# Hybrid GDN and retention block: GpSimd issues the stores of the latent chunks' preparation and of the adaLN rows

## The chip, the cores and the metric

One Trainium2 chip, one of its cores. The metric is the device time of one execution in microseconds; the time of a kernel is the median of its runs. Engines are called as in the profile: PE is TensorE (PEld its weight loads), DVE is VectorE, ACT is ScalarE, POOL is GpSimd, SP is SyncE, which does no arithmetic and only issues transfers (SPq is its queue).

## What is computed

One layer of a diffusion transformer over 256 context and 1024 latent tokens with 1024 features in float32. Cut to what matters here:

```
p = modulate(rms_norm([ctx; x])) @ w_in            # adaLN: shift, scale, gate from silu(c) @ W + b
q, k, v = silu(short_conv(p))                       # 4 heads of 128: gated DeltaNet (GDN)
decay[i, j] = exp(G[i] - G[j])        for i >= j    # G: running sum of the log decays in a chunk
A = strict_lower(beta_i * (k_i . k_j) * decay)      # per chunk, head and direction
u, w = solve(I + A, [beta v, beta k exp(G)])        # the triangular solve of each chunk
qk = (q_i . k_j) * decay ;  q_dec = q * exp(G)      # "scores" of the chunk
scan over chunks, forwards and backwards:  v_new = u - w S ;  o = q_dec S + qk v_new ;  S = ...
y = [GDN out ; retention out], gated ;  x += g1 * (y @ w_out)
x += g2 * swiglu(modulate(rms_norm(x))) ;  out = rms_norm(x)
```

The reference uses chunks of 64, the kernel chunks of 128 tokens; context chunks need no scores, since only latent tokens are put out.

## The kernel before

Products run on PE as three matmuls of float32 operands that are split into a high and a low part (whi, wlo; ACT L344 makes the high part, DVE or POOL L345 the low part). A scheduler orders the instructions of each engine when the program is built: each engine then works through its queue strictly in that order, and waits at an instruction until the semaphores it needs are there. All transfers that SP, ACT and POOL issue stand in their queues among the other instructions.

The program goes through these stages: adaLN and the norms; the in-projection, part of it with tokens on the partitions (`token_major`, matmuls L371 to L373), and for GDN's k, q and v with channels on the partitions (`conv_block`, L607 to L624, its convolution on DVE L621); then, per chunk of 128 tokens, the preparation and the triangular solves; the scan (`step`, first matmuls L922); retention; the out-projection; the feed-forward part; the last norm.

The change is in two places. `ada_rest` (L488) runs beside the projections of q and k, one call a head: SP loads the weights (L495), DVE accumulates, and for the two gate rows g1 and g2 SP loads a bias row (L503), DVE adds (L505), and SP stores 512 elements to the DRAM tile `grow` (L506). The row is read again much later, at 681 us (g1) and 1293 us (g2).

`pre(t)` (L700) prepares chunk t; there are 10, 0 and 1 of the context, 2 to 9 latent. Chunk rows kc and qc are loaded by SP (L664). PE makes kk = k k' and kq = k q' in PSUM. For each of two directions d, SP loads the decay row broadcast over the partitions (gw, L718), POOL masks it (e, `affine_select`, L722), ACT takes exp (L726), DVE multiplies kk by e into ut (L730) and, for latent chunks, kq by e into half of sp (L732). SP stores ut (128x512, 256 KB) to the DRAM tile un of its batch (L733). For latent chunks ACT takes exp of gw (L735), POOL multiplies it by qc into the other half of sp (L736), and SP stores sp (512 KB) to the scan's DRAM tile sd (L737). The tiles gw, e, ut and sp have two buffers each, so a store must have landed before DVE or POOL may write the tile again two directions later.

`BATCH = [[0,1,2,9],[3,8,4,7],[5,6]]` gives three batches of chunks. After the chunks of a batch, `invert(b)` (L743) inverts the 32x32 diagonal blocks: SP loads them from un into yr (L751), ACT and DVE copy them into L (L758, L759), DVE does 31 steps of a product and a subtraction (L765, L767) in series, copies a transpose (L769), and SP stores the results to xd (L771). `merge(b)` (L801) then builds the whole inverses: SP loads un into U (L783) and the diagonal blocks from xd into U (L787) and t64 (L788), PE multiplies (L807, L814, L817, L830, L834) with copies by DVE between (xt1 L810, xt2 L831) and by ACT. ACT stores U to sd (L838). The program text calls solve(0), solve(1) (preparation and inversion of batches 0 and 1), the convolution of v with its transposes (PE L856, ACT L859 into vt of two buffers, ACT store L860), the preparation of batch 2, merge(0), the load of the rope tables (L872), invert(2), merge(1), merge(2), and two `token_major` groups (8, 9), whose matmuls fill PE in this stage. The scheduler interleaves all of these.

```
for d in range(2):
    ...
    V.tensor_tensor(ut ..., pk, e ..., ALU.mult)                       # L730
    if t >= 2:
        V.tensor_tensor(sp[:, 0] ..., pq, e ..., ALU.mult)             # L732
    SY.dma_start(un[b][:, 1 - d, c * H:(c + 1) * H, :], ut)            # L733
```

Of the kernel before, what the change touches and what calls it, by code (L numbers as in the profile page):

```python
# [25 lines left out]
H = 4  # L26
# [12 lines left out]
def build(nc, tc, ap, dbg=None, stop=None, marks=None):  # L39
    root = ExitStack()  # L40
    V, S, G, T, SY = nc.vector, nc.scalar, nc.gpsimd, nc.tensor, nc.sync
# [51 lines left out]
    def bank_b(name):  # L93
        return bank("pb", name)
# [47 lines left out]
    def softplus(pl, x, n, tag):  # L142

        a = pl.tile([P, n], F32, tag=tag + "a", name=tag + "a")
        s = pl.tile([P, n], F32, tag=tag + "s", name=tag + "s")
        q = pl.tile([P, n], F32, tag=tag + "q", name=tag + "q")
        V.scalar_tensor_tensor(a, x, -1.0, x, ALU.mult, ALU.max)
        S.activation(a, a, AF.Exp, scale=-1.0)
        V.tensor_scalar(s, a, 2.0, None, ALU.add)
        V.reciprocal(s, s)  # L150
        V.tensor_tensor(s, s, a, ALU.mult)
        V.tensor_tensor(q, s, s, ALU.mult)
        V.tensor_scalar(a, q, 1.0 / 19.0, None, ALU.mult)
        for k in (17, 15, 13, 11, 9, 7, 5, 3):
            V.scalar_tensor_tensor(a, a, 1.0 / k, q, ALU.add, ALU.mult)
        V.scalar_tensor_tensor(a, a, 1.0, s, ALU.add, ALU.mult)
        V.tensor_scalar(s, x, 0.0, None, ALU.max)
        V.scalar_tensor_tensor(s, a, 2.0, s, ALU.mult, ALU.add)
        return s
# [31 lines left out]
    try:  # L191
# [293 lines left out]
        grow = [dr.tile([1, D], F32, tag="grow%d" % i, name="grow%d" % i) for i in range(2)]  # L485

        def ada_rest(c, half):

            c0 = c * D + half * 512
            src = ap["ada2"][2 * (c - 2) + half]  # L490
            acc = R2.tile([P, 512], F32, tag="acc", name="acc", bufs=1)
            for k in range(KT):
                if k % 2 == 0:
                    w = R2.tile([P, 2, 512], F32, tag="adaw2", name="adaw2", bufs=2)
                    SY.dma_start(w, src[k // 2])  # L495
                if k == 0:
                    V.tensor_scalar(acc, w[:, 0], csl[:, k, 0:1], None, ALU.mult)
                else:
                    V.scalar_tensor_tensor(acc, w[:, k % 2], csl[:, k, 0:1], acc, ALU.mult, ALU.add)
            ps = bank_b("gr")  # L500
            if c in (2, 5):
                row = R2.tile([1, 512], F32, tag="row", name="row", bufs=1)
                SY.dma_start(row, ap["adarow"][c0:c0 + 512].unsqueeze(0))  # L503
                T.matmul(ps[:1, :], ones[:, 0:1], acc, start=True, stop=True)
                V.tensor_tensor(row, row, ps[:1, :], ALU.add)  # L505
                SY.dma_start(grow[0 if c == 2 else 1][:, half * 512:(half + 1) * 512], row)  # L506
            else:
                for k in range(4):
                    T.matmul(ps[:, 2 * k:2 * k + 2], acc[:, k * P:(k + 1) * P], ones[:, 0:2], start=True, stop=True)
                ks = slice(half * 4, half * 4 + 4)  # L510
                o = ada2[:, c - 3, ks]
                V.tensor_tensor(o, ps[:, 0:8].rearrange("p (k t) -> p k t", t=2)[:, :, 0],
                                adab[:, 8 * c + 4 * half:8 * c + 4 * half + 4], ALU.add)
                if c == 4:
                    V.scalar_tensor_tensor(o, o, 1.0, gffn[:, ks], ALU.add, ALU.mult)
# [19 lines left out]
        for g in range(2):  # L535
            ada_rest(2, g)
# [13 lines left out]
        sd = dr.tile([TT, P, 10, 512], F32, tag="sd", name="sd")  # L550
# [4 lines left out]
        def c8(t, d):  # L555
            return slice(t * 8 + d * 4, t * 8 + d * 4 + 4)
# [11 lines left out]
        sp = softplus(AB, av.rearrange("p a n -> p (a n)"), 2 * TT * 8, "sp")  # L568
# [3 lines left out]
        sp = sp[:, :TT * 8]  # L572
# [82 lines left out]
        for h in range(H):  # L655
            y = newy()
            conv_block(4 + h, y, False)
            ada_rest(3 + h // 2, h % 2)
            S.dma_start(kd[:, :, h, :].rearrange("t p j -> p t j"), y.rearrange("p (t j) -> p t j", j=P))
            kstat(h, y)  # L660

        def load(pl, src, tag, bufs, shape=(P, H, P)):
            x = pl.tile(list(shape), F32, tag=tag, name=tag, bufs=bufs)
            SY.dma_start(x, src)  # L664
            return x
# [11 lines left out]
        for h in range(H):  # L677
            y = newy()
            conv_block(h, y, True)
            if h < 2:  # L680
                ada_rest(5, h)
            S.dma_start(qd[:, :, h, :].rearrange("t p j -> p t j"),
                        y[:, NCTX:].rearrange("p (t j) -> p t j", j=P))
# [14 lines left out]
        un = [dr.tile([P, 2, len(ch) * H, P], F32, tag="un%d" % b, name="un%d" % b) for b, ch in enumerate(BATCH)]  # L698

        def pre(t):  # L700
            b, c = where[t]
            kc = load(GP, kd[t], "kc", 2)
            pk = bank_b("kk")
            for h in range(H):
                T.matmul(pk[:, h * P:(h + 1) * P], kc[:, h, :], kc[:, h, :], start=True, stop=True)
            if t >= 2:
                qc = load(GP, qd[t - 2], "qc", 2)
                pn = bank_b("qt")
                for h in range(H):
                    T.transpose(pn[:, h * P:(h + 1) * P], qc[:, h, :], ident)  # L710
                for h in range(H):
                    S.activation(pn[:, h * P:(h + 1) * P], pn[:, h * P:(h + 1) * P], AF.Square, accum_out=nq[:, t - 2, h:h + 1])
                pq = bank_b("kq")
                for h in range(H):
                    T.matmul(pq[:, h * P:(h + 1) * P], kc[:, h, :], qc[:, h, :], start=True, stop=True)
            for d in range(2):
                gw = GP.tile([P, H, P], F32, tag="gw", name="gw", bufs=2)
                SY.dma_start(gw.rearrange("p h i -> p (h i)"),  # L718
                             grow_d[c8(t, d), :].rearrange("a b -> (a b)").partition_broadcast(P))
                e = GP.tile([P, H, P], F32, tag="e", name="e", bufs=2)  # L720
                sg = 1 if d == 0 else -1
                G.affine_select(out=e, in_=gw, compare_op=ALU.is_ge, fill=FAR, base=0,  # L722
                                pattern=[[0, H], [sg, P]], channel_multiplier=-sg)
                for h in range(H):
                    col = t * 8 + d * 4 + h
                    S.activation(e[:, h, :], e[:, h, :], AF.Exp, bias=sm["nG"][:, col:col + 1])  # L726
                if t >= 2:
                    sp = GP.tile([P, 2, H, P], F32, tag="sp", name="sp", bufs=2)
                ut = GU.tile([P, H, P], F32, tag="ut", name="ut", bufs=2)
                V.tensor_tensor(ut.rearrange("p h i -> p (h i)"), pk, e.rearrange("p h i -> p (h i)"), ALU.mult)  # L730
                if t >= 2:
                    V.tensor_tensor(sp[:, 0].rearrange("p h i -> p (h i)"), pq, e.rearrange("p h i -> p (h i)"), ALU.mult)  # L732
                SY.dma_start(un[b][:, 1 - d, c * H:(c + 1) * H, :], ut)  # L733
                if t >= 2:
                    S.activation(gw, gw, AF.Exp)  # L735
                    G.tensor_tensor(sp[:, 1], gw, qc, ALU.mult)  # L736
                    SY.dma_start(sd[t, :, 8 - 8 * d:10 - 8 * d], sp.rearrange("p a h i -> p a (h i)"))  # L737

        q32 = [slice(32 * k, 32 * k + 32) for k in range(4)]

# [100 lines left out]
        def solve(b):  # L841
            for t in BATCH[b]:
                pre(t)
            checkpoint("pre%d" % b)
            invert(b)
            checkpoint("inv%d" % b)
# [19 lines left out]
        for t in BATCH[2]:  # L866
            pre(t)
# [787 lines left out]
```

## Time and profile before

| what | value |
|---|---|
| time, median of 3 runs | 1476.58 us (1475.48 to 1484.42) |
| the profiled execution | 1477.96 us, its span 1476.2 us |
| busy share of the span | PE 95%, PEld 81%, DVE 65%, ACT 42%, POOL 40% |
| transfers that the change moves | un 20 x 256 KB, sd scores 16 x 512 KB, grow 4 x 2 KB |
| median from issue to landing | un 3.4 us, sd 5.2 us, gw loads 4.8 us |
| the chunk stage in the trace | first ut at 277.5 us, scan's first matmuls at 473.5 us |

The profile is one execution, taken by the hardware profiler. The span runs from its first to its last instruction; the device time is a little longer. Of a view of the timeline each row has the start in us, the duration in us, engine, line, operation, and in brackets how long the engine had been idle and what released it. `x4` behind a row means four instructions in a row of that kind. Windows of time give the busy time of each engine inside them. Register and semaphore work isn't counted as busy.

### The profile page before, as it was taken

The numbers are of one execution on the slowest core, as the hardware profiler recorded it, in microseconds if no ns is written. First come the engines' busy times: TensorE is split into PE (matmuls) and PEld (weight loads), VectorE is DVE, ScalarE is ACT, GpSimd is POOL, SyncE is SP. The second block draws the span as 40 slices with busy tenths as digits, with TensorE's granted clock in tenths as the row PEclk, the third lists the DMA queues.
The fourth block names the chain that finished last, engine by engine and source line by source line (L and its number), as shares of the span: only waits on it lengthen the run. The fifth ranks groups of instructions, "written<-read, shape, count | busy, mean of one in ns | idle before, by whom it ended". The sixth has DMA issues, their size and how long they took to land.

```text
span 1476.2 us, 24111 instructions
## 1 busy us (share of the span) xinstructions
PE 1397.2 (95%) x8919; PEld 1199.2 (81%) x8919; DVE 964.6 (65%) x1856; ACT 614.0 (42%) x1326; POOL 590.3 (40%) x501
## 2 busy tenths in 40 slices
PE   7999999986789999899799899999999999999997
PEld 2898888975689999898688688877888888788885
DVE  6566789289792435689676877556555564657477
ACT  5643564587333111245443623233333332444445
POOL 0120010243202344234144688898555552335321
PEclk9999999998899999999899999999999999999999
DMA  9536686688888625996532265674222242776863
GB/s 337 197 105 205 189 249 200 219 264 277 282 216 277 238 76 178 416 341 209 184 125 104 97 238 210 242 264 162 105 97 105 107 151 79 260 260 194 288 216 114
DMA packets 170421, 298.14 MB, mean 202 GB/s; under 512 B 43496, under 2 KB 93880, under 8 KB 165952
## 3 DMA queue, kind: packets, MB, share of 16 engines
q1 hardware_dynamic: 118752, 253.17, 50.2%
q10 hardware_dynamic: 49072, 35.83, 7.8%
q0 software_dynamic: 2480, 7.60, 1.4%
q8 instruction: 70, 1.15, 0.3%
q14 instruction: 47, 0.39, 0.1%
HBM read 206.60 MB, written 89.96 MB: 201 GB/s over the span
## 4 chain that ended last, share of the span: by engine, by line
PE 55%; POOL 6%; DMA 5%; DVE 4%; issue 2%; ACT 2%; SPq 1%; ACTq 0%; POOLq 0%; DVEq 0%
PE ffn L1344 7%; PE ffn L1342 6%; PE ffn L1343 6%; PE fo L1470 4%; PE fo L1469 4%; PE fo L1468 4%; PE tm L371 3%; PE tm L373 3%; PE tm L372 3%; PE op L1203 2%; PE op L1201 2%; PE op L1202 2%; DMA wd<-tw 2%; POOL ws L1315 1%; DMA pk<-sd 1%
## 5 line engine op out<-in xcount | busy, mean ns | idle before, releaser
L371 PE MATMUL tm<-whi,hhi 128*128 128x256 f32 (+1 forms) x704 | 199.5, 287 | 7.7 <-ACT vt L859 3.4
L372 PE MATMUL tm<-wlo,hhi 128*128 128x256 f32 (+1 forms) x704 | 199.3, 285 | 2.4 <-issue 2.0
L373 PE MATMUL tm<-whi,hlo 128*128 128x256 f32 (+1 forms) x704 | 197.7, 285 | 0.0
L371 PEld LDWEIGHTS tm<-whi,hhi 128*128 128x128 f32 x704 | 132.8, 190 | 11.8 <-ACT vt L859 3.6
L1342 PE MATMUL ffn<-t,whi 128*128 128x512 f32 x352 | 136.9, 390 | 1.3 <-ACT whi L344 1.3
L1344 PE MATMUL ffn<-t,wlo 128*128 128x512 f32 x352 | 137.0, 390 | 1.0 <-DVE wlo L345 1.0
L1343 PE MATMUL ffn<-t,whi 128*128 128x512 f32 x352 | 137.0, 389 | 0.0
L372 PEld LDWEIGHTS tm<-wlo,hhi 128*128 128x128 f32 x704 | 133.7, 190 | 2.1 <-issue 0.9
L373 PEld LDWEIGHTS tm<-whi,hlo 128*128 128x128 f32 x704 | 132.8, 190 | 2.6 <-issue 1.8
L344 ACT ACTIVATE whi<-wraw 128x512 fp32r<-128x512 f32 (+2 forms) x98 | 75.1, 771 | 141.4 <-PE ffn L1343 80.5
L344 ACT ACTIVATE whi<-ws 128x512 fp32r<-128x512 f32 x88 | 55.6, 632 | 171.5 <-PE ffn L1343 123.4
L345 DVE TENSOR_TENSOR wlo<-ws,whi 128x512 fp32r<-128x512 f32 x88 | 93.9, 1068 | 47.0 <-ACT whi L344 46.8
L1469 PE MATMUL fo<-wlo,ahi 128*128 128x512 f32 x308 | 120.2, 390 | 2.1 <-DVE wlo L345 2.1
L1468 PE MATMUL fo<-whi,ahi 128*128 128x512 f32 x308 | 119.3, 390 | 0.7 <-ACT ahi L344 0.7
L1470 PE MATMUL fo<-whi,alo 128*128 128x512 f32 x308 | 119.0, 390 | 0.0
L345 DVE TENSOR_TENSOR wlo<-wraw,whi 128x512 fp32r<-128x512 f32 (+2 forms) x92 | 99.4, 1082 | 24.6 <-ACT whi L344 24.6
L1342 PE MATMUL ffn<-b,whi 128*128 128x512 f32 x264 | 103.8, 393 | 4.4 <-ACT whi L344 4.4
L1344 PE MATMUL ffn<-b,wlo 128*128 128x512 f32 x264 | 103.6, 393 | 0.8 <-DVE wlo L345 0.8
L1343 PE MATMUL ffn<-b,whi 128*128 128x512 f32 x264 | 103.4, 392 | 0.0
L612 PE MATMUL b<-hlo,whi 128*128 128x512 f32 (+1 forms) x256 | 94.4, 369 | 0.0
L613 PE MATMUL b<-hhi,wlo 128*128 128x512 f32 (+1 forms) x256 | 94.3, 368 | 0.0
L611 PE MATMUL b<-hhi,whi 128*128 128x512 f32 (+1 forms) x256 | 94.3, 368 | 0.0
(446 smaller groups left out, 3448.1 us busy)
## 6 DMA issues: line engine op xcount, KB each, us to landing
adaw<-ada SPq DMA_DIRECT2D x48, 512.0 KB, 4.4
pk<-sd SPq DMA_DIRECT2D x16, 1536.0 KB, 10.0
wraw<-wfi SPq DMA_DIRECT2D x44, 512.0 KB, 3.7
ar<-ad SPq DMA_DIRECT2D x33, 512.0 KB, 4.7
w<-wfo SPq DMA_DIRECT2D x22, 512.0 KB, 5.7
wd<-tw SPq DMA_DIRECT2D x11, 1024.0 KB, 4.8
ad<-act SPq DMA_DIRECT2D x20, 512.0 KB, 3.0
raw<-wd SPq DMA_DIRECT2D x20, 512.0 KB, 4.9
```

What stands on the lines that cost most here:

```text
L344: S.activation(hi, raw, AF.Copy)
L345: e.tensor_tensor(lo, raw, hi.bitcast(F32), ALU.subtract)
L371: T.matmul(o, hhi[:, k, tsl], whi[:, k % 4, :], start=(k == 0), stop=False)
L372: T.matmul(o, hhi[:, k, tsl], wlo[:, k % 4, :], start=False, stop=False)
L373: T.matmul(o, hlo[:, k, tsl], whi[:, k % 4, :], start=False, stop=(k == KT - 1))
L612: T.matmul(o, whi[:, k, :], hl, start=False, stop=False)
L1342: T.matmul(o, whi[:, k, :], xhi(xn, slice(0, 4), k), start=(first and k == 0), stop=False, **kw)
L1343: T.matmul(o, whi[:, k, :], xlo(xn, slice(0, 4), k), start=False, stop=False, **kw)
L1344: T.matmul(o, wlo[:, k, :], xhi(xn, slice(0, 4), k), start=False, stop=(k == 3), **kw)
L1468: T.matmul(po[g][i], ahi[:, ts], whi, start=(j == 0 and not kw), stop=False, **kw)
L1469: T.matmul(po[g][i], ahi[:, ts], wlo, start=False, stop=False, **kw)
L1470: T.matmul(po[g][i], alo[:, ts], whi, start=False, stop=(j == FH - 1), **kw)
```

## The change

The store of the adaLN gate rows (L506) is issued by GpSimd. In `pre`, the store of ut stays on SP only for the two context chunks; for the eight latent chunks it is issued by GpSimd behind its product into sp, and so is the store of sp: 16 stores of 256 KB, 16 of 512 KB and 4 of 2 KB. No arithmetic, tile or number of buffers changes. Line numbers from L738 on grow by two, and L736 becomes L737.

```
-                SY.dma_start(grow[0 if c == 2 else 1][:, half * 512:(half + 1) * 512], row)
+                G.dma_start(grow[0 if c == 2 else 1][:, half * 512:(half + 1) * 512], row)
...
-                SY.dma_start(un[b][:, 1 - d, c * H:(c + 1) * H, :], ut)
-                if t >= 2:
+                if t < 2:
+                    SY.dma_start(un[b][:, 1 - d, c * H:(c + 1) * H, :], ut)
+                else:
                     S.activation(gw, gw, AF.Exp)
                     G.tensor_tensor(sp[:, 1], gw, qc, ALU.mult)
-                    SY.dma_start(sd[t, :, 8 - 8 * d:10 - 8 * d], sp.rearrange("p a h i -> p a (h i)"))
+                    G.dma_start(un[b][:, 1 - d, c * H:(c + 1) * H, :], ut)
+                    G.dma_start(sd[t, :, 8 - 8 * d:10 - 8 * d], sp.rearrange("p a h i -> p a (h i)"))
```

Since the order of every queue is made anew when the program is built, instructions that the diff doesn't touch move too, all of them between the start of the chunk stage and the scan. Three places matter below. The number behind a name tells apart the tiles of one name.

**POOL, at the end of batch 0.** e_3045 and e_3063 are the masks of chunk 9's two directions, e_3215 and e_3233 those of the next chunk (3), sp its products; before:

```order
L722 AFFINE_SELECT e_3045<-gw_3043 128x512
L736 TENSOR_TENSOR sp_3053<-gw_3043,qc_3027 128x512
L722 AFFINE_SELECT e_3063<-gw_3061 128x512
L736 TENSOR_TENSOR sp_3071<-gw_3061,qc_3027 128x512
L722 AFFINE_SELECT e_3215<-gw_3213 128x512
L722 AFFINE_SELECT e_3233<-gw_3231 128x512
```

And with the change:

```order
L722 AFFINE_SELECT e_3045<-gw_3043 128x512
L722 AFFINE_SELECT e_3063<-gw_3061 128x512
L737 TENSOR_TENSOR sp_3053<-gw_3043,qc_3027 128x512
L738 DMA un0_2892<-ut_3054 128x512
L739 DMA sd_1296<-sp_3053 128x1024
L737 TENSOR_TENSOR sp_3071<-gw_3061,qc_3027 128x512
L722 AFFINE_SELECT e_3215<-gw_3213 128x512
L738 DMA un0_2892<-ut_3072 128x512
L739 DMA sd_1296<-sp_3071 128x1024
L722 AFFINE_SELECT e_3233<-gw_3231 128x512
```

The second mask of chunk 9 now stands ahead of the first product, and the last store of batch 0 (ut_3072, which the loads of yr wait for) stands behind the first mask of chunk 3. On SP the decay rows gw_3061 and gw_3231 move up, each directly behind the row of the other direction, since the stores between them are gone.

**SP, where the first inversion's results are stored and merge(0) begins.** U0 and U1 are the tiles of merge(0) and merge(1), xd0 the first inversion's results, yr_4440 the third inversion's input; before:

```order
L783 DMA U1_4550<-un1_2893 128x4096
L771 DMA xd0_3079<-X_3086 64x1024 x2
L771 DMA xd0_3079<-XT_3184 64x1024 x2
L751 DMA yr_4440<-un2_2894 16x32x32 x3
L783 DMA U0_4175<-un0_2892 128x4096
L872 DMA rope_4049<-rope 128x1280
L751 DMA yr_4440<-un2_2894 16x32x32
L788 DMA t64_4177<-xd0_3079 32x32x32 x4
L787 DMA U0_4175<-xd0_3079 32x32x32 x4
```

And with the change:

```order
L785 DMA U1_4550<-un1_2893 128x4096
L785 DMA U0_4175<-un0_2892 128x4096
L773 DMA xd0_3079<-X_3086 64x1024
L773 DMA xd0_3079<-XT_3184 64x1024
L773 DMA xd0_3079<-X_3086 64x1024
L773 DMA xd0_3079<-XT_3184 64x1024
L874 DMA rope_4049<-rope 128x1280
L753 DMA yr_4440<-un2_2894 16x32x32 x4
L789 DMA U0_4175<-xd0_3079 32x32x32 x3
L790 DMA t64_4177<-xd0_3079 32x32x32 x3
```

The 2 MB load of U0 moves up past the stores of xd0 and the loads of yr_4440, directly behind U1's.

**DVE, in the second inversion.** Its steps are the pairs on X_3433; xt1_4252 is merge(0)'s copy between its first and second products; before:

```order
L765 TENSOR_TENSOR tmp_3504<-L_3432,X_3433 128x207
L767 TENSOR_TENSOR X_3433<-X_3433,tmp_3504 128x9x23
L810 TENSOR_SCALAR xt1_4252<-m1_4187 128x512
L765 TENSOR_TENSOR tmp_3507<-L_3432,X_3433 128x192
L767 TENSOR_TENSOR X_3433<-X_3433,tmp_3507 128x8x24
```

And with the change:

```order
L767 TENSOR_TENSOR tmp_3522<-L_3432,X_3433 128x87
L769 TENSOR_TENSOR X_3433<-X_3433,tmp_3522 128x3x29
L767 TENSOR_TENSOR tmp_3525<-L_3432,X_3433 128x60
L769 TENSOR_TENSOR X_3433<-X_3433,tmp_3525 128x2x30
L812 TENSOR_SCALAR xt1_4252<-m1_4187 128x512
L767 TENSOR_TENSOR tmp_3528<-L_3432,X_3433 128x31
L769 TENSOR_TENSOR X_3433<-X_3433,tmp_3528 128x31
```

xt1 moves seven steps later in the second inversion. On PE, the matmuls of merge(0) that need it (L814 before) now stand behind 17 more matmuls of `token_major`.

## The prediction

> **What bounds the kernel now.** I began with the page's table of engines, to see which engine the whole span belongs to, and then cut the neighbourhood of the change into stretches (columns: stretch, its length, busy time with number of instructions for PE, PEld, DVE, ACT, POOL, then the granted clock, the share of the DMA engines and GB/s).
>
> ```profile
> PE 1397.2 (95%) x8919; PEld 1199.2 (81%) x8919; DVE 964.6 (65%) x1856; ACT 614.0 (42%) x1326; POOL 590.3 (40%) x501
> 100.00:300.00 200.00, 200.00 (x1229) 175.52 (x1228) 142.79 (x244) 99.70 (x275) 23.33 (x20) 1.00 0.68 215
> 285.00:375.00 90.00, 68.70 (x409) 58.94 (x407) 77.08 (x108) 74.20 (x210) 38.87 (x33) 0.92 0.84 264
> 300.00:380.00 80.00, 58.65 (x342) 50.44 (x341) 70.92 (x110) 64.58 (x179) 33.56 (x27) 0.89 0.86 270
> 380.00:400.00 20.00, 16.62 (x141) 16.41 (x140) 13.81 (x36) 4.01 (x10) 3.49 (x4) 1.00 0.92 311
> 400.00:480.00 80.00, 72.22 (x1527) 68.56 (x1526) 49.95 (x131) 24.22 (x44) 8.76 (x18) 0.98 0.87 243
> 480.00:580.00 100.00, 100.00 (x855) 99.85 (x855) 42.25 (x130) 10.92 (x14) 43.47 (x86) 1.00 0.43 157
> ```
>
> PE is the engine of the span, at 95%, and it has no gap from 100 to 300 us nor from 480 to 580 us. What is saved there on any other engine is worth nothing. Between 300 and 480 us PE idles 21.4 + 3.4 + 7.8 = 32.5 us. This is where the stores sit that the change moves, and it is the most that it could give back. From 300 to 380 us DVE is busy 70.92 of 80 us: it is the limit there, because the 31-step inversions stand on it. Where the scan starts (its first L922 at 473.52, quoted in part 5) PE is full again, so I let each us by which the stage ends later or earlier carry through to the end one to one.
>
> Next I read who the moved instructions wait for (us in all, times, longest), and what one issue costs on either queue (least, median and most ns).
>
> ```profile
> SPq L733 <- DVE ut L730: 29.2, 16, 4.3
> SPq L737 <- DVE sp L732: 8.1, 10, 2.8
> SPq L506 <- DVE row L505: 23.5, 4, 15.8
> L733 SPq DMA_DIRECT2D un<-ut x20: 319/320/736, 278.2 to 374.2; - x20
> L737 SPq DMA_DIRECT2D sd<-sp x16: 319/320/428, 289.6 to 374.8; - x16
> L506 SPq DMA_DIRECT2D grow<-row x4: 246/247/252, 116.6 to 261.8; - x4
> L387 POOL DMA_DIRECT2D rd<-res x36: 557/557/738, 458.1 to 583.1; - x36
> ```
>
> **Part 1: the issues themselves.** SP loses 16 x 0.32 + 16 x 0.32 + 4 x 0.25 = 11.2 us of issuing and the waits for DVE behind which its loads stood. POOL gets 36 issues. What these shapes cost from POOL the trace doesn't show; the nearest row is L387, 0.56 us for rows of half the length, and I take that, so 36 x 0.56 = 20.2 us, 17.9 of them for the 32 stores of the latent chunks. The bounds are SP's own 0.32 (10.2 us for the 32) and twice L387 for the doubled rows (35.8 us). From 285 to 375 us POOL is busy 38.87 of 90 us, so 51 us are free, and I cost the issues at 0; what they cost without that cover is the second rival. The four row stores end 23.5 us of waits of SP, whose next adaLN weight loads stood behind; PE is full there, so 0.
>
> **Part 2: the first inversion, on the last store of batch 0.** Here are SP, POOL and DVE around it (start, duration, instruction, and in brackets the idle time before it with its releaser).
>
> ```profile
> 290.62 1.26 SPq L718 DMA_DIRECT2D gw<-grow_d  x1
> 296.59 0.45 SPq L718 DMA_DIRECT2D gw<-grow_d  x1
> 301.43 0.32 SPq L733 DMA_DIRECT2D un<-ut  x1
> 304.06 4.49 SPq L751 DMA_DIRECT2D yr<-un  x4
> 294.85 1.29 POOL L736 TENSOR_TENSOR sp<-gw,qc 128x512 f32<-128x512 f32 x1 [1.98 <-ACT gw L735]
> 298.19 1.12 POOL L722 TENSOR_SCALAR_AFFINE_SELECT e<-gw 128x512 f32<-128x512 f32 x1 [2.04 <-DMA gw<-grow_d]
> 303.54 0.64 POOL L722 TENSOR_SCALAR_AFFINE_SELECT e<-gw 128x512 f32<-128x512 f32 x1 [0.98 <-DMA gw<-grow_d]
> 308.69 0.69 DVE L730 TENSOR_TENSOR ut<-kk,e 128x512 f32<-128x512 f32 x1 [3.73 <-ACT e L726]
> 311.99 1.47 DVE L759 COPY L<-yr 64x1024 f32<-64x1024 f32 x1
> ```
>
> The store at 301.43 is chunk 9's second, the last that the inversion's loads (304.06) need; the inversion begins at 311.99. In the new order POOL runs both masks of chunk 9 first, then the product, and the last store stands behind the mask of the next chunk, e_3215. That mask needs a decay row whose load can only be issued when the product at 294.85 has freed its buffer. The row loads come free of the two score stores ahead of them, but the second one still waits for its buffer: issued about 290.1 rather than 290.62, it lands between 295 and 298. So the product runs at 296 to 299.3 and the next row load at 297.4 to 300.6, against 296.59. With the 4.8 to 6.9 us that these loads take here (296.59 to 303.54 is 6.9) the mask is done at 302.8 to 308, and the last store goes out then: 1.4 to 6.6 us after 301.43. DVE's own chunk at 308.69 waits on the same masks. Bounds of this term: 0 (DVE's order hides it) and +6.7. I take +3, nearer the lower half, since SP's queue ahead of 304.06 is emptier than before.
>
> **Part 3: stalls that the row loads may lose.** Later row loads no longer stand behind stores. DVE's last wait on a mask before the second batch ends is this one:
>
> ```profile
> 369.74 0.69 DVE L730 TENSOR_TENSOR ut<-kk,e 128x512 f32<-128x512 f32 x1 [1.95 <-ACT e L726]
> ```
>
> I take all of it, -2; bounds -2 and 0.
>
> **Part 4: the 2 MB load of U0.** The views are SP's timeline and the chain of waits (start, duration, what).
>
> ```profile
> 391.78 0.56 SPq L783 DMA_DIRECT2D U<-un  x1
> 389.32 0.20 DVE L765 TENSOR_TENSOR tmp<-L,X 128x31 f32<-128x31 f32 x1 [5.03 <-ACT L L758]
> 385.83 1.14 ACT L859 ACTIVATE vt<-vT,svy 128x128 f32<-128x128 f32 x4 [7.78 <-DMA sd<-vt]
> 376.44 9.31 DMA sd<-vt
> 395.35 7.89 SPq L788
> 406.62 5.18 DMA U<-xd
> 411.85 0.22 PE m L814 x2
> ```
>
> In the new order this load stands right behind U1's and goes out near 378 us, not at 391.78. The 7.89 us in which SP waits inside the diagonal loads then go, and merge(0) has its data some 8 us earlier; part 5 says why this is worth 0. But two 2 MB loads are then in flight beside the v store that takes 9.31 us, for which ACT's third vt copy waits 7.78 us, and behind that copy on ACT stands L758, for which DVE waits 5.03 us before the second inversion. The four MB and the v stores at the 311 GB/s of 380 to 400 us take 4.5 MB / 311 = 14.5 us, ending near 391, against 385.83: up to +5 on DVE's restart, 0 if the small store gets its share first. I take +2.
>
> **Part 5: xt1 seven steps later.** merge(0)'s second product (L814) needs xt1, which stands in DVE's queue in the midst of the second inversion.
>
> ```profile
> 409.58 0.68 DVE L810 TENSOR_SCALAR xt<-m 128x512 f32<-128x512 f32 x1
> 414.54 0.22 DVE L767 TENSOR_TENSOR X<-X,tmp 128x60 f32<-128x60 f32 x1
> 469.96 0.12 PE tm L373
> 473.52 1.98 PE Tr L922 x16
> ```
>
> Now it stands behind the step that ends at 414.76 here; less its own 0.60 it would run at 414.16 and end at 414.84, so L814 moves from 411.85 by +3.0. PE's order has 17 more projection matmuls ahead of that point, 17 x 0.12 = 2.0 us done in the gap that need not be done later. Net +1.0; bounds +1.0 and +3.0. This order also caps part 4: however early U0 lands, L814 follows the inversion.
>
> **The sum.** 0 + 3 - 2 + 2 + 1 = +4.0, with ends at -1 and +14.7. The terms come from the profiled execution of 1477.96 us (span 1476.2 and what lies around it), 1.4 above the median; its forecast is 1482.0, and on the median 1476.58 + 4.0 = 1480.6 us.
>
> **The rivals.** First, **no path changes**: the masks keep pace, the vt store isn't slowed, and xt1's shift is filled by PE: 1476.6 us. For it speaks that SP is nowhere the bound; against it that DVE's order has changed at points it waits on. The Trainium skill's page "DMA: Bandwidth & Descriptors", section "Issuing engines are not separate DMA queues", has a rule that comes to this result: another issuing engine saves only the sequencer's issue time.
>
> Second, slower: **POOL becomes the ring of the chunk loop.** The waits for DVE move with the stores: SP sat 29.2 + 8.1 = 37.3 us on them, and every later mask would now stand behind those. 38.87 + 17.9 + 37.3 = 94.1 us is more than the 90 us in which all this must fit; it decides if these waits don't overlap with POOL's present idling for row loads. A mask behind a store delays ACT's exp, then ut, then the next store. Then the issues are paid in full: 1476.6 + 17.9 = 1494.5 us. Against it: POOL's idle time now is mostly waiting for the same chunk's rows and exps.
>
> Third, faster: **SP's freedom is passed on.** Row loads and U0 come early enough that DVE's waits 3.73, 1.95 and 5.03 us all go, less the 1.0 of part 5: -9.7, or 1466.9 us. For it: each is a wait at the end of a load that SP issues late. Against it: part 2's buffers and the vt store.
>
> Fourth, **DVE and POOL block each other at every issue.** These rows show that engines do block (x2 is two instructions):
>
> ```profile
> 1263.00 3.59 DVE L345 TENSOR_TENSOR alo<-ar,ahi 128x512 fp32r<-128x512 f32 x2
> 1269.91 1.28 DVE L345 TENSOR_TENSOR alo<-ar,ahi 128x512 fp32r<-128x512 f32 x2
> 1263.02 1.30 POOL L1381 TENSOR_TENSOR sx<-act 128x512 f32<-128x512 f32 x1
> 1269.39 0.57 POOL L1384 DMA_DIRECT2D ad<-act  x1
> 1269.95 0.53 POOL L1386 DMA_DIRECT2D ad<-sx  x1
> ```
>
> Beside a POOL product two DVE operations take 3.59 us, beside two POOL issues 1.28 us. If the 32 issues blocked as products do, (3.59 - 1.28) / 2 = 1.15 us each, DVE would lose 36.8 us: 1513.4 us. The last three rows speak against it, as neither side is stretched. The Trainium skill ("SBUF — State Buffer", section "Who interferes with whom") warns against just this change, as a DMA from GpSimd can't write its descriptors while DVE runs a copy, cast or tensor_scalar in a two-port mode; it excepts tensor_tensor, with which the last rows agree. By that rule L759's 1.47 us at 311.99 is all that could block a store here, some 1.5 us of POOL's time, and no run yet shows it.
>
> **How the numbers follow.** Chances: the forecast 0.52, no path changed 0.16, POOL's ring 0.13, SP's freedom 0.13, blocking 0.06. The forecast's own range is 1475.6 to 1491.3 us (the ends of the sum); the rivals of both signs widen it to 1466 to 1495, which leaves out the fourth and the far tails. One per cent, about what a measurement of this kernel tells from no change, is 14.8 us: below 1461.8 only the third rival overshooting, 0.05; above 1491.3 the second and fourth, with part of their chances given up to milder forms, 0.14; the rest 0.81.
>
> **What would show it.** In the new profile: POOL's issues at 0.5 to 0.6 us; the first L to be copied from yr at 313 to 318 rather than 311.99; no wait of SP inside the diagonal loads; the third vt copy at 386 to 391; L814 some 5 us or more after 411.85; the first L922 near 478 instead of 474 us. Wrong: masks that wait for a store's DVE operand over and over (the second rival, shown by POOL idle before L738 and L739 of 20 us or more that DVE also idles), an inversion that starts before 312 (the third), or DVE steps stretched beside POOL issues (the fourth). A shift outside 285 to 480 us would overthrow the frame itself.

## The result

The changed kernel took 1500.7 us (median of 4 runs, 1498.44 to 1501.74) beside 1476.03 us for the kernel before. The ratio is 1.0148, with a 95% interval of 1.0128 to 1.0168: 21.9 us more (0.0148 x 1476). The forecast of 1480.6 us and the range up to 1495 us were too low.

Stretches of the changed kernel, with the columns of the prediction's first fence:

```profile
PE 1406.9 (94%) x8919; PEld 1209.1 (81%) x8919; DVE 968.5 (65%) x1856; ACT 616.7 (41%) x1328; POOL 610.8 (41%) x537
100.00:300.00 200.00, 200.00 (x1231) 175.65 (x1230) 141.51 (x242) 102.96 (x278) 26.29 (x27) 1.00 0.68 212
285.00:375.00 90.00, 70.11 (x400) 60.05 (x398) 69.12 (x94) 64.89 (x180) 47.67 (x55) 0.93 0.74 234
300.00:380.00 80.00, 57.93 (x314) 49.06 (x313) 65.24 (x90) 57.64 (x163) 42.96 (x49) 0.88 0.76 236
380.00:400.00 20.00, 8.83 (x58) 8.62 (x58) 13.77 (x31) 6.60 (x16) 6.56 (x7) 0.67 0.89 338
400.00:480.00 80.00, 65.31 (x1162) 62.74 (x1162) 52.85 (x136) 22.63 (x42) 4.08 (x5) 0.84 0.65 163
```

PE is still full up to 300 us. From 300 to 480 us it now idles 22.1 + 11.2 + 14.7 = 48.0 us instead of 32.5, in a stage that also ends later. DVE is no longer full from 300 to 380 us (65.24 instead of 70.92 us of 80) and does little more in all (968.5 against 964.6 us): its work waited. PE was also slower. For the same 8919 matmuls it is busy 9.7 us longer (1406.9 against 1397.2), at a granted clock of 0.67 instead of 1.00 from 380 to 400 us and of 0.84 instead of 0.98 from 400 to 480 us. So of the 23.7 us by which the span grew 14.0 are more idle time of PE and 9.7 are slower matmuls. Cut into pieces of 20 us, the stage has its lowest clock in both kernels where PE has least to do: before from 360 to 380 us (busy 8.94 us, 0.62), now from 380 to 400 us (8.83 us, 0.67). These are the rows that answer to the prediction's (POOL, SP, DVE, ACT, the chain of waits):

```profile
300.41 1.29 POOL L737 TENSOR_TENSOR sp<-gw,qc 128x512 f32<-128x512 f32 x1 [2.16 <-DMA sd<-sp]
305.32 0.64 POOL L722 TENSOR_SCALAR_AFFINE_SELECT e<-gw 128x512 f32<-128x512 f32 x1 [1.22 <-DMA gw<-grow_d]
305.91 0.60 POOL L738 DMA_DIRECT2D un<-ut  x1
310.40 3.77 SPq L753 DMA_DIRECT2D yr<-un  x4
322.45 1.08 DVE L761 COPY L<-yr 64x1024 f32<-64x1024 f32 x1 [9.73 <-DMA yr<-un]
392.30 1.12 DVE L771 COPY XT<-X 128x1024 f32<-128x1024 f32 x1
385.78 1.91 SPq L785 DMA_DIRECT2D U<-un  x2
386.30 17.13 DMA sd<-vt
403.51 0.37 ACT L861 ACTIVATE vt<-vT,svy 128x128 f32<-128x128 f32 x1 [15.61 <-DMA sd<-vt]
406.69 0.21 DVE L767 TENSOR_TENSOR tmp<-L,X 128x31 f32<-128x31 f32 x1 [12.20 <-ACT L L760]
432.88 0.69 DVE L812 TENSOR_SCALAR xt<-m 128x512 f32<-128x512 f32 x1 [1.25 <-PE m L809]
433.93 1.12 DVE L771 COPY XT<-X 128x1024 f32<-128x1024 f32 x1
436.33 0.21 PE L816 MATMUL m<-U,xt 32*32 32x32 f32 x1
441.86 0.26 PE L816 MATMUL m<-U,xt 32*32 32x32 f32 x2 [3.59 <-issue]
L924 PE MATMUL Tr<-pk x16: 275/275/377, 501.3 to 504.5; 128*128 128x128 f32 x16
```

From these and the same rows of before the lateness can be followed along the stage. XT is the copy that ends an inversion.

| point | before | after | later by | added on the way |
|---|---|---|---|---|
| yr copied, first inversion begins | 311.99 | 322.45 | 10.5 | 10.5 |
| first inversion's XT | 381.01 | 392.30 | 11.3 | 0.8 |
| second inversion's XT | 415.24 | 433.93 | 18.7 | 7.4 |
| scan's first matmuls | 473.4 | 501.3 | 27.9 | 9.2 |
| end of the span | 1476.2 | 1499.9 | 23.7 | -4.2 |

So three legs lost 11.3, 7.4 and 9.2 us, and 4.2 came back behind the scan's start. The experiments were to tell two theories apart. By theory A the loss lies in three places of the queues (the last store of batch 0, U0's load, xt1). By theory B it is the price of issuing 32 stores from GpSimd, and scales with their number. In what follows a time in us against before is the ratio's excess times 1476, and the brackets behind a ratio are its 95% interval.

### The profile page after: what moved, and what is told of

It is laid out like the page before. It is cut to its first block, busy times and chain, and to the rows that moved or that the text cites. A ratio compares the mean times of both kernels' runs of the same rounds, so it can differ in the third digit from the quotient of the medians.

```text
span 1499.9 us, 24114 instructions
## 1 busy us (share of the span) xinstructions
PE 1406.9 (94%) x8919; PEld 1209.1 (81%) x8919; DVE 968.5 (65%) x1856; ACT 616.7 (41%) x1328; POOL 610.8 (41%) x537
## 4 chain that ended last, share of the span: by engine, by line
PE 54%; POOL 6%; DMA 5%; DVE 5%; issue 2%; ACT 2%; SPq 0%; ACTq 0%; POOLq 0%; DVEq 0%
PE ffn L1346 6%; PE ffn L1344 6%; PE ffn L1345 6%; PE fo L1470 4%; PE fo L1472 4%; PE fo L1471 4%; PE tm L372 3%; PE tm L371 3%; PE tm L373 3%; PE op L1205 2%; PE op L1203 2%; PE op L1204 2%; DMA wd<-tw 2%; DMA sd<-vt 1%; PE up L931 1%
## 5 line engine op out<-in xcount | busy, mean ns | idle before, releaser
L371 PE MATMUL tm<-whi,hhi 128*128 128x256 f32 (+1 forms) x704 | 202.3, 291 | 14.2 <-ACT vt L861 11.2
L372 PE MATMUL tm<-wlo,hhi 128*128 128x256 f32 (+1 forms) x704 | 202.3, 289 | 3.7 <-DVE wlo L345 3.7
L345 DVE TENSOR_TENSOR wlo<-ws,whi 128x512 fp32r<-128x512 f32 x88 | 94.1, 1070 | 47.6 <-ACT whi L344 47.4
L345 DVE TENSOR_TENSOR wlo<-wraw,whi 128x512 fp32r<-128x512 f32 (+2 forms) x92 | 99.1, 1079 | 23.8 <-ACT whi L344 23.6
## 6 DMA issues: line engine op xcount, KB each, us to landing
pk<-sd SPq DMA_DIRECT2D x16, 1536.0 KB, 11.3
```

The lines of the kernel that those rows point to most:

```text
L345: e.tensor_tensor(lo, raw, hi.bitcast(F32), ALU.subtract)
L371: T.matmul(o, hhi[:, k, tsl], whi[:, k % 4, :], start=(k == 0), stop=False)
L372: T.matmul(o, hhi[:, k, tsl], wlo[:, k % 4, :], start=False, stop=False)
```

## The experiments

**1 to 4: parts of the change.** The edits, on the kernel before (first) and the changed one:

```
1  (G if t == 9 else SY).dma_start(un[b]..., ut)        # before, two stores on GpSimd
2  SY.dma_start(sd[t, ...], sp ...)                     # changed, score stores back on SP
3  SY.dma_start(un[b]..., ut)                           # changed, stores of ut back on SP
4  if t < 2 or t == 9: SY.dma_start(un[b]..., ut)       # changed, chunk 9's back on SP
```

> The kernel before with only two stores issued by GpSimd: those of ut of chunk 9, the last of batch 0. In POOL's queue the second stands behind the next chunk's first mask, as in the changed kernel; U0's load keeps its old place and xt1 stands three steps earlier. Queue places (theory A: the loss comes from three places in the queues, the last store of batch 0 first): the store goes out 2 to 5 us after the 301.4 of before, the first inversion's copy from yr starts 2 to 6 us after 312.0, and the kernel takes +1 to +6 us. Issuing (theory B: each store that GpSimd issues costs, 24 us for 32 stores): 2 of 32, +1.5 us, and the copy from yr stays within 1 us of 312.

> The changed kernel with the score stores back on SP: GpSimd issues the 16 stores of ut and the four row stores. The last store of batch 0 now stands ahead of the next chunk's mask in POOL's queue, and U0's load stands behind the stores of xd0. Theory A: first inversion 0 to 4 us after 312, the v store that ACT waits for lands in 9 to 11 us, +2 to +9 us in all against before. Theory B: half of the stores, +12 us.

> The changed kernel with all stores of ut back on SP: GpSimd issues the 16 score stores (twice the bytes of the others) and the four row stores. The loads of yr stand directly behind the last store of batch 0 on SP; U0's load stands behind the stores of xd0. Theory A: first inversion within 4 us of 312, v store 9 to 11 us, xt1 late as in the changed kernel, 0 to +8 us. Theory B: half the stores or two thirds of the bytes, +12 to +16 us.

> The changed kernel with only the two stores of ut of chunk 9 back on SP; 30 chunk stores stay on GpSimd. In this order both loads of U0 and U1 stand behind the stores of xd0, so no 2 MB load is in flight with the v store, and xt1 stands early. Theory A: the first inversion starts within 4 us of 312, the v store lands in under 10 us, and the time is +0 to +8 us against before. Theory B: 30 of 32 stores, +22 us.

Measured: 1.0026 [1.0006, 1.0047], 1.0058 [1.0041, 1.0074], 1.0068 [1.0043, 1.0093] and 1.0075 [1.0049, 1.0101], that is +3.8, +8.6, +10.0 and +11.1 us. Theory B fails on the second and the fourth, for which it said +12 and +22 us; on the first its +1.5 us lies inside the interval, but it had the copy from yr within 1 us of 312. Theory A's ranges of time hold for the first two and, by the measured ratio, are exceeded by the third and fourth (+8 us at most, which both intervals still reach); its ranges for the copy are exceeded in all four. Along the stage the four are alike: DVE copies yr at 319.1, 317.0, 318.3 and 316.4 us, and ends the first inversion at 386.6, 387.5, 387.9 and 385.2 us instead of 381.0. Two stores alone were enough for much of the late start. Experiment 4 has no 2 MB load beside the v store, but U1's load stands between merge(0)'s two sets of diagonal loads, and its first xt2 waits 6.12 us for PE.

**5: the swap that I had held for the cause.** One edge puts chunk 3's mask behind the last store of batch 0; no other row moved on any engine.

```
+                with tc.issue_after(last_un[9]) if t == 3 else nullcontext():
                     G.affine_select(out=e, in_=gw, ...)
```

> The changed kernel with one swap in POOL's queue and nothing else moved on any engine: the last store of batch 0 stands ahead of the first mask of chunk 3 (all 36 stores stay on GpSimd). As the changed kernel's trace reads, the store then goes out at 304.1 instead of 305.9, since the product ahead of it still waits until 300.4 for a score store to land: the first inversion starts 2 us earlier (320.5 instead of 322.4), and the time is +19 to +21 us against before. If the mask were the whole cause of the late inversion, it would start at 312 to 314 and the time would be +11 to +13 us. If issuing alone costs (theory B), +22 us, as in the changed kernel.

Measured: 1.0108 [1.0092, 1.0124], +15.9 us. POOL, SP and DVE of its profiled execution:

```profile
303.88 0.60 POOL L741 DMA_DIRECT2D un<-ut  x1
309.63 3.98 SPq L756 DMA_DIRECT2D yr<-un  x4
322.19 1.05 DVE L764 COPY L<-yr 64x1024 f32<-64x1024 f32 x1 [9.90 <-DMA gw<-grow_d]
```

The store went out 2.0 us earlier and the copy began 0.3 us earlier: in this execution the mask is not what makes the inversion late. The time fits none of the three expectations. It is 6 us below the changed kernel's, which doesn't show in this execution, the longest of its runs (1498.69 of 1493.82 to 1498.69); where these 6 us come from stays open.

**6 to 8: the places of U0's load and xt1, and ACT's wait.**

```
6  with tc.issue_after(stored[0]): SY.dma_start(uu..., un[0])     # U0 behind the stores of xd0
7  5 and 6, and xt1 queued ahead of the second inversion's step 192 (its product of 128x192)
8  vt = CV.tile([P, 4, P], F32, tag="vt", name="vt", bufs=4)
```

> The changed kernel with the load of U0 put behind the stores of xd0 on SP (all 36 stores stay on GpSimd; the scheduler moves a few rows around it). Queue places (theory A): the v store lands in 9 to 11 us instead of 17.1, ACT's third vt copy runs near 396 instead of 403.5, the second inversion starts 6 to 8 us earlier, and the time is +14 to +17 us against before. Theory B: +22 us.

> The changed kernel with three places put back, all 36 stores on GpSimd: the last store of batch 0 ahead of chunk 3's mask, U0's load behind the stores of xd0, and xt1 of merge(0) ahead of the second inversion's step 192, where it stood before. Theory A: -2, -7 and -3 to -5 us together, +8 to +13 us against before; the rest is the score stores that land later. Theory B: +22 us.

> The changed kernel with four buffers for vt instead of two, so that ACT's third vt copy needs no landed v store; U0's load stays right behind U1's. Theory A: ACT's 15.6 us of waiting go, the second inversion starts at 394 to 397 instead of 406.7, and the time is +10 to +15 us against before (merge(0) still waits for U0's blocks behind the slow v stores). Theory B: +22 us.

Measured: 1.0144 [1.0129, 1.0159], 1.0073 [1.0046, 1.0099], 1.0082 [1.0065, 1.0099]: +21.3, +10.8 and +12.1 us. Experiments 7 and 8 came out as theory A had them. 6 did not (+14 to +17 us), and its time is theory B's, though the third vt copy ran at 397.85 us, near the 396 expected. DVE and SP of experiment 6:

```profile
392.37 1.12 DVE L772 COPY XT<-X 128x1024 f32<-128x1024 f32 x1
402.14 0.52 SPq L774 DMA_DIRECT2D xd<-X  x1
```

The scheduler had moved the load of the rope tables ahead of the stores of xd0, where its wait held them for 9.8 us. The edit had bought one late place with another, so it doesn't price U0's place. Experiments 13 and 14 mend that. Its scan starts at 494.9 us, 6.4 us before the changed kernel's, and yet it takes the same time: the scan's start isn't the time. In the profiled executions of the sixteen experiments the span is up to 7.0 us less late than the scan's start (16: 2.5 and 9.5 us) and up to 2.3 us more (13: 21.5 and 19.2 us).

**9 and 10: another issuing engine; the row stores alone.**

```
9   S.dma_start(un[b]..., ut);  S.dma_start(sd[t, ...], sp ...)     # changed kernel, ACT issues
10  G.dma_start(grow[...], row)                                     # before, nothing else
```

> The changed kernel with the 32 stores of the latent chunks issued by ACT instead of GpSimd; SP has only loads there as in the changed kernel, and U0's load stands behind the stores of xd0. Theory G (the late first inversion, 322.4 instead of 312.0, comes from GpSimd's own queue of transfers, in which a store of ut lands behind two score stores): yr is copied at 312 to 316, and the time is 0 to +6 us against before. Theory F (it comes from taking the stores out of SP's queue, so that the decay row loads overtake them and the stores land later, whoever issues them): yr is copied at 317 to 321, +7 to +12 us. ACT's 32 issues of some 0.37 us lie in a stretch where ACT is busy 74 of 90 us; up to +5 us may be added by that in both.

> The kernel before with the four row stores alone issued by GpSimd; the chunk stage keeps its order on every engine. All theories: -1 to +1 us, since PE has no gap there.

Measured: 1.0022 [1.0009, 1.0034], +3.2 us, and 0.9987 [0.9973, 1.0001], no difference. With ACT issuing, SP is as free as in the changed kernel, and the first inversion ends at 383.99 us, 3.0 late instead of 11.3; here xt1 and U0's load also stand in better places. The yr copy began at 317.88 us, as theory F said, but behind convolution work that the new order put ahead of it: the last store of batch 0 had gone out at 300.32 us, earlier than before, and the loads of yr were issued by 309.22 us. The end of the inversion is the fairer mark, though it was chosen after the run, and it speaks for theory G. The time lies in theory G's range too, but the better places have a part in it.

**11, 12 and 16: the same places with no store moved.** The kernel before with four vt buffers, alone (11), with U0's load and xt1 held (12), and with the loads of U0 and rope held (16).

> The kernel before with four buffers for vt (no store moved). ACT's third vt copy needs no landed store, so DVE's 5.03 us of waiting before the second inversion go; but the scheduler now puts U0's load right behind U1's and xt1 seven steps later, as in the changed kernel. Theory A (those two places cost the changed kernel some 5 us and more each): -2 to +4 us. If the places cost nothing: -5 us.

> The kernel before with four buffers for vt, U0's load held behind the stores of xd0 and xt1 held ahead of the second inversion's step 192. Theory A: the 5.03 us of DVE's wait are kept, -3 to -6 us against before, and 2 to 8 us less than the same kernel without the two places held. If the places cost nothing, both kernels take the same time.

> The kernel before (no store moved) with four buffers for vt and the loads of U0 and rope held behind the stores of xd0; xt1 stands five steps later than before. A candidate that might beat both. Theory A: DVE's 5.03 us before the second inversion go, the late xt1 and 15 matmuls fewer ahead of the scan (1.8 us) give 3 to 5 back: -3 to +2 us, and 5 to 9 us less than the eleventh run. If the places cost nothing: +7 us like the eleventh.

Measured: 1.0048 [1.0031, 1.0066], 1.0061 [1.0044, 1.0077] and 1.0019 [1.0002, 1.0036]: +7.1, +9.0 and +2.8 us. Theory A's ranges are missed by 11 and 12, and by 16 narrowly. An edit that only takes a wait away cost 7 us; the scheduler then put U0's load, with rope behind it, ahead of the stores of xd0, and xt1 1.9 us ahead of the second inversion's XT instead of 5.7. DVE and SP of experiment 11:

```profile
384.22 1.13 DVE L769 COPY XT<-X 128x1024 f32<-128x1024 f32 x1
397.42 0.51 SPq L771 DMA_DIRECT2D xd<-X  x1
417.51 0.69 DVE L810 TENSOR_SCALAR xt<-m 128x512 f32<-128x512 f32 x1 [0.52 <-PE m L807]
419.37 1.12 DVE L769 COPY XT<-X 128x1024 f32<-128x1024 f32 x1
```

The results of the first inversion lie 13 us before SP stores them. In 12 xt1 had its early place (421.43, XT at 426.69 us), but rope's load moved ahead of the stores of xd0 (396.64, XT at 387.44 us), and DVE stood 7.69 and 1.39 us at two low parts (L345) ahead of xt1, waiting for ACT. So 11 and 12 take the same time within their intervals, as if the places cost nothing, and 12 doesn't price them. With both loads held (16) 4.3 us of the 7.1 return, with intervals that overlap a little. None of the three beats the kernel before, and neither does any other here beyond its interval.

**13 and 14: both loads held, then xt1 too, all 36 stores on GpSimd.**

```
+            with tc.issue_after(stored[0]): ... SY.dma_start(uu ..., un[0])
+        with tc.issue_after(stored["U", 0]): SY.dma_start(rope, ap["rope"])
14: + tc.add_manual_dep(step_of[1, 23], xt1_inst.name, ...NoSync...)
```

> The changed kernel with the loads of U0 and of the rope tables both held behind the stores of xd0 on SP, as in the kernel before (in the sixth run the rope load had moved ahead of those stores and kept them back until 402 us). All 36 stores stay on GpSimd, xt1 late. Theory A: v store in 9 to 11 us instead of 17, stores of xd0 right after the first inversion (393 to 397), scan start 6 to 9 us before the changed kernel's 501.3, and +14 to +17 us against before (PE's order has 24 projection matmuls fewer ahead of the scan, 2.9 us). If the place of these loads costs nothing: +22 us.

> The thirteenth run's kernel with xt1 also held ahead of the second inversion's step 192. Theory A: scan start another 3 to 5 us earlier (488 to 491), +8 to +12 us against before: what is left is the late first inversion. If xt1's place costs nothing: the same time as the thirteenth run.

Measured: 1.0128 [1.0106, 1.0149] and 1.0076 [1.0055, 1.0097]: +18.9 and +11.2 us. In 13 the v store takes 12.08 us instead of 17.13, and the scan starts at 492.6 instead of 501.3 us; three of those 8.7 us are time in which 24 projection matmuls fewer were done, and in time it gives 3.0 us, with intervals that overlap, so the time alone doesn't show it. The trace does: from the first XT to the second (390.60 to 425.92) it takes 35.3 us, against 34.2 before and 41.6 in the changed kernel. xt1's place gives another 7.7 us of time. In 14 the last leg, from the second XT (429.24) to the scan's start (488.0), takes 58.8 us, against 66.7 in 13, 67.4 in the changed kernel and 58.2 before. What remains in 14 is the late first inversion (XT at 392.04) and 3.0 us of the second leg.

**15: issues or bytes?**

```
-  G.dma_start(sd[t, :, 8 - 8 * d:10 - 8 * d], sp ...)
+  G.dma_start(sd[t, :, 8 - 8 * d:10 - 8 * d, :64], sp ...[:, :, :64])
```

> The changed kernel with the same 36 issues on GpSimd, but the 16 score stores write only 64 of 512 elements of each row, 64 KB instead of 512 KB; the output is then not the reference's, as the scan reads placeholder scores that SP writes long before (8 MB beside the projections of k). The last store of batch 0 stands ahead of chunk 3's mask, as in the fifth run; U0 and xt1 stand as in the changed kernel. Theory L (the late first inversion comes from stores that land late in a full set of DMA engines): yr is copied at 311 to 316 us, the first inversion ends 8 us or more before the changed kernel's 392.3, and the time is +2 to +9 us. Theory P (it comes from what an issue costs in POOL's queue, 0.6 us each and the waits in its order): yr is copied at 319 or later, +13 to +18 us.

Measured: 1.0096 [1.0070, 1.0122], +14.2 us. Here are SP and DVE of it:

```profile
279.90 1.29 DVE L736 TENSOR_TENSOR ut<-kk,e 128x512 f32<-128x512 f32 x2 [13.90 <-PE kk L711]
308.92 2.86 SPq L759 DMA_DIRECT2D yr<-un  x4
315.42 1.45 DVE L767 COPY L<-yr 64x1024 f32<-64x1024 f32 x1
384.41 1.12 DVE L777 COPY XT<-X 128x1024 f32<-128x1024 f32 x1
397.79 0.51 SPq L779 DMA_DIRECT2D xd<-X  x1
```

The stage starts 2.1 us later than in the changed kernel (its first ut there was at 277.82 us), yet yr is copied at 315.42 instead of 322.45 us: with the issues kept and most of the bytes gone, 7.0 of the 10.5 us of lateness vanish, or 9.1 if the later start is taken off. The copy is in theory L's range, and the first inversion ends 7.9 us before the changed kernel's (it had 8 or more). The time lies in theory P's range: this order has rope ahead of the stores of xd0 again (397.79, 13 us after XT) and xt1 late. Its second and third legs take 38.1 and 66.4 us, against 41.6 and 67.4 in the changed kernel.

The first leg can be cut in three, at the last store of batch 0, at the end of SP's issuing of the loads of yr that wait for it, and at the copy:

| kernel | last store goes out | loads of yr issued by | copy begins | last two apart |
|---|---|---|---|---|
| before | 301.43 | 308.55 | 311.99 | 3.4 |
| changed | 305.91 | 314.17 | 322.45 | 8.3 |
| 5, store ahead of the mask | 303.88 | 313.61 | 322.19 | 8.6 |
| 15, store ahead of the mask, small score stores | 303.96 | 311.78 | 315.42 | 3.6 |

Of the 10.5 us, 4.5 are there when the store goes out, 1.1 are added up to the last issue, and 4.9 in the landing of the loads. (Before and in 15 DVE didn't wait at the copy, so there the loads took at most 3.4 and 3.6 us.) What lies beside the loads is the difference: before, SP issued the next chunk's first stores behind them, and in the changed kernel POOL issues them beside them. SP before, POOL after:

```profile
309.41 0.33 SPq L733 DMA_DIRECT2D un<-ut  x1
310.52 0.32 SPq L737 DMA_DIRECT2D sd<-sp  x1
```

```profile
310.94 0.60 POOL L738 DMA_DIRECT2D un<-ut  x1
311.54 0.54 POOL L739 DMA_DIRECT2D sd<-sp  x1
```

In 15 the score stores among these are small, and they go out only from 313.31 us, behind the loads; which of the two shortens the landing isn't separated.

The time from issue to landing between 286 and 305 us, in the views of the transfers of before, of the changed kernel and of experiment 9 (count, size, median us):

```profile
sd<-sp SPq DMA_DIRECT2D x4, 512.0 KB, 5.1
un<-ut SPq DMA_DIRECT2D x4, 256.0 KB, 3.2
gw<-grow_d SPq DMA_DIRECT2D x4, 256.0 KB, 5.2
```

```profile
sd<-sp POOLq DMA_DIRECT2D x3, 512.0 KB, 8.7
gw<-grow_d SPq DMA_DIRECT2D x4, 256.0 KB, 3.5
un<-ut POOLq DMA_DIRECT2D x3, 256.0 KB, 4.2
```

```profile
sd<-sp ACTq DMA_DIRECT2D x4, 512.0 KB, 7.8
un<-ut ACTq DMA_DIRECT2D x4, 256.0 KB, 4.0
gw<-grow_d SPq DMA_DIRECT2D x4, 256.0 KB, 5.4
```

In this stretch a score store lands in 5.1 us on SP and in 8.7 on GpSimd, while the row loads that used to stand behind it land in 3.5 instead of 5.2. These are three or four transfers each. Over the whole stage the 16 score stores have the same median on both queues, but a longer tail on GpSimd (SP before, GpSimd after):

```profile
DMA to landing us min/median/max: 2.6/5.2/6.7
DMA to landing us min/median/max: 3.0/5.2/12.2
```

With two buffers of sp the slow stores are at once on the path: POOL's product at 300.41 us waits 2.16 us for the store of two directions ago, the next row load waits for that product, and so on to the store at 305.91 us. On ACT's queue the score stores take 7.8 us and the row loads gain nothing (5.4 us), and yet the last store goes out early (300.32 us); why the inversion then ends only 3 us late, whether by GpSimd's 0.6 us at each issue or by the different order, isn't separated.

## Why the prediction was wrong, point by point

**The frame held.** PE stays full up to 300 us, the loss lies in the chunk stage, and of its 27.9 us 23.7 arrived at the end, though other runs show that this is not one to one. The losses lie where parts 2, 4 and 5 looked for them. Their sizes failed, all to the same side, and part 2 had left out a wait.

**Part 1 held:** GpSimd's issues cost 0.53 to 0.62 us (0.56 forecast) and the issues of the rows nothing (experiment 10).

```profile
L738 POOL DMA_DIRECT2D un<-ut x16: 547/598/617, 289.1 to 385.3; - x16
L739 POOL DMA_DIRECT2D sd<-sp x16: 533/539/597, 291.6 to 386.2; - x16
POOL un L738 <- DVE ut L730: 12.2, 6, 4.4
SPq L718 <- POOL sp L737: 44.4, 11, 8.3
```

**Part 2 failed:** +3 us, at most +6.7, against 10.5. It had the mechanism half right. I followed the order of the rows and priced each transfer by its landing on SP's queue before. The last store went out 4.5 us late, inside my 1.4 to 6.6. On the way there I had missed that a score store could land so late that the two buffers of sp put it in front of the next row load (the last row above: SP's row loads now wait 44.4 us for POOL's products). The step that broke the bound is the next one: I let the inversion follow the last store at the old distance, but the last load of yr landed 8.3 us after SP had issued it, instead of 3.4 at most, amid the next chunk's stores. The mask in front of the last store, on which I built the term, gave 0.3 us in the profiled execution of experiment 5. Part 3's gain of 2 us isn't seen: the wait at the row it named is gone, but DVE's waits for ACT's exp are 6.9 us in the stage instead of 7.0, and from the copy to XT the first inversion takes 0.8 us more.

**Part 4 was mis-sized:** +2, at most +5, against 7.4 for the second leg. U0's load did go out beside the v store of 128 KB, which took 17.13 us with 4 MB of loads beside it instead of 9.31; with U0 and rope held (experiment 13) it took 12.08, and 6.3 of the 7.4 us went. I had reckoned 14.5 us from the mean rate of a whole stretch. That merge(0) would have its data earlier was wrong too: by the profile's waits, SP's stores of xd0 now stood 12.8 us for the same v stores, instead of 4.0.

**Part 5 was mis-sized:** +1.0, against 9.2 for the third leg, of which experiment 14 gave 7.7 us of time back by moving xt1 alone. xt1 was 5.7 us ahead of the second inversion's XT before (409.58, 415.24) and 1.05 us after (432.88, 433.93), which is 4.6 of the 9.2 us. The products behind it, PE before:

```profile
410.66 0.21 PE L814 MATMUL m<-U,xt 32*32 32x32 f32 x1
411.85 0.22 PE L814 MATMUL m<-U,xt 32*32 32x32 f32 x2 [0.93 <-DMA U<-xd]
```

Before, the first of them ran 0.4 us after xt1 had ended; now (436.33) 2.8 us after it, behind projection matmuls that PE took one after the other, 0.12 us each. That is 2.4 us more. I had booked the 17 added matmuls as a gain of 2.0 us; on the path they were a further wait. The remaining 2.2 us come later. PE stops once more for 3.59 us inside these products (to 441.86), for a reason that the profile doesn't show.

**The rivals.** POOL's ring, which gave 1494.5 us, was nearest in number and wrong in kind: POOL waits 12.2 us for DVE at L738 rather than 37.3, and is busy 47.67 of 90 us. The fourth fell: no issue is stretched. The first rival's time, 1476.6 us, is missed by 3.2 us with ACT issuing (experiment 9) and by 21.9 with GpSimd, both with new orders. In the Trainium skill, page "DMA: Bandwidth & Descriptors", section "SWDGE vs HWDGE vs iDMA", it is said that the two kinds of descriptor queue feed different queues inside each transfer engine, which are served in turn. The landing times between 286 and 305 us (5.1 to 8.7 us for the stores, 5.2 to 3.5 us for the loads) agree with that; the equal medians over the whole stage don't show it.

## What to carry to other kernels

A store moved to another queue is not only an issue moved: it no longer stands in line with the loads of the old queue. Ask which loads it will now run beside (here 128 KB loads that took 8.3 us instead of 3.4), and, if its tile has two buffers, who waits for that tile. Where a scheduler builds the queues anew, read the whole diff of the order for every instruction that a long wait could catch, and price each one; in experiment 11 a new order cost 7 us with no store moved at all. And where the order of transfers changes, landing times of the kernel before are no upper bound: parts 2, 4 and 5 had 6.7, 5 and 3 us as theirs, and measured 10.5, 7.4 and 9.2.

## What the hardware showed that I had not expected

A store of vt of 128 KB took 17.13 us beside two loads of 2 MB, while one of 256 KB took 2.3 us at a quieter time: what else was in flight counted for more than its size. In the stretch in which PE idled most its granted clock was lowest too, and 9.7 of the 23.7 us were slower matmuls. And an issue by GpSimd didn't go by bytes: 0.54 us for 512 KB, 0.60 for 256 KB, 0.72 for the 64 KB of experiment 15, which come in shorter rows.
